# A Conformer and delta-rule trunk on one core: the second convolution's last Pool tile goes to VectorE, and the final norms' 1/rms is made with tokens on partitions

## The chip, the cores and the metric

The kernel runs on one core of a Trainium2 chip. The metric is the device time of one execution in microseconds (us), of the only core. Before the change it is 2406.96 us, the median of three runs (2406.86 to 2407.51).

## What is computed

A two-layer trunk over 1024 tokens of width 1024, all in float32. Layer 0 mixes tokens with a Conformer convolution module, layer 1 with a gated delta rule; each layer ends in a squared-ReLU MLP of width 4096, and a last RMS norm gives the output. Cut to the parts that the change touches:

```python
def conformer_conv(h, w_pw1, b_pw1, w_dw, b_dw, ln_g, ln_b, w_pw2, b_pw2):
    u = h @ w_pw1 + b_pw1
    u = jax.nn.glu(u, axis=-1)
    u = causal_depthwise_conv(u, w_dw) + b_dw
    u = jax.nn.silu(layer_norm(u, ln_g, ln_b))
    return u @ w_pw2 + b_pw2
def sqrelu_mlp(h, w1, w2):
    return jnp.square(jax.nn.relu(h @ w1)) @ w2
...
    return rms_norm(h, final_norm_g)
```

The depthwise convolution has 31 taps per channel; `rms_norm` multiplies by `rsqrt(mean(x*x) + eps)`, taken over the 1024 channels of a token.

## The kernel before

Activations lie with channels on partitions: a tensor of 512 tokens (one half `hf` of the sequence) is eight tiles of 128 channels by 512 tokens, counted by `ct`, `o` or `k`. Every matrix product is made in three passes for accuracy: weights and activations are each split into a high part and a low rest. `weights` (L161, L162) loads a raw 128x1024 block of weights, ScalarE copies it to `wh` (L161) and VectorE makes the rest `wl` (L162). `product` then issues, for each of eight k, a matmul of `wh` with the high activations (L201), of `wh` with the low ones (L202) and of `wl` with the high ones (L203): 24 matmuls. `wh` and `wl` have two buffers each (`WB = 2`), and blocks are prepared two products ahead (`AHEAD = 2`), so the block for product n+2 can be made only when product n has been issued through to its end.

Work that is not a product runs as Python generators behind the products; `tick()` advances them. The Tile scheduler turns this into one fixed order of instructions per engine, and each engine keeps to its order: an instruction that waits holds all behind it.

The second half's convolution (`hf = 1`) runs behind the MLP of layer 0, first half. That MLP is four quarters q of eight products into the hidden layer (`m1_00_q0` to `m1_00_q7`, in `mlp_hid`) and eight out of it (`m2_00_q0` to `m2_00_q7`, in `mlp_out`). After an `m1` product ScalarE takes ReLU, square and the high part (L591, L592, L102) and VectorE the low rest (L103); after an `m2` product VectorE scales (L622) and adds (L365).

The table `CONV` says which engine makes each of the eight convolution tiles. `"v"` is `conv_vec`: one multiply on VectorE (L510), then 30 fused multiply-adds (L517), as tiles `ca` and `c`. `"p"` is `conv_pool`: one ScalarE step, then 30 pairs on Pool of a multiply (L441) and an add (L446), as tiles `cv` and `cp`. The second number is the pace: how many taps between two yields. In half 1, tiles 0, 1 and 7 are Pool's. A finished tile is added to a running sum `ln1` (`conv_done`, L424).

`layer_norm(1, ...)` (from L531) starts when all eight tiles are done: mean by a matmul over the channels (`mean_lnm1`), eight subtractions on VectorE (L540), squares on ScalarE (L272) added up on Pool (L543), the variance by a matmul (`lnv1`, L548), square root on ScalarE (L247), a 128x512 reciprocal on VectorE (L248), eight products with it, four on VectorE (L560) and four on Pool (L558), fifteen or sixteen silu steps on ScalarE (L568, L569), and the split (L570). The first half's layer norm does the reciprocal in another form: `add_stats` (L254) puts tokens on partitions, so that square root and reciprocal work on 128x4 elements, and `rstd_of_tokens` brings the result back with a broadcast copy (L264) and four transposes (L267).

`final` makes the last norm: for the first half of the tokens over 512 columns, for the second half over two pieces of 256. Squares (L1006, L1010), mean by two matmuls (L1012, L1013), square root (L1016), reciprocal (L1017), then eight products and eight output DMAs. In the last piece, tiles 1, 4 and 7 go through ScalarE (L1022) and Pool (L1024), the others through VectorE (L1026).

Of the kernel before, what the change touches and what calls it, by code (L numbers as in the profile page):

```python
# [7 lines left out]
F32 = mybir.dt.float32  # L8
# [6 lines left out]
P = 128  # L15
# [15 lines left out]
        (("p", 1), ("p", 1), ("v", 3), ("v", 1), ("v", 1), ("v", 3), ("v", 1), ("p", 3)))  # L31
# [22 lines left out]
def _body(ctx, tc, a, out):  # L54
# [196 lines left out]
    def add_stats(ps, x, first=True, last=True):  # L251

        for t in range(NCH):
            nc.tensor.matmul(ps[:, t:t + 1], x[:, t * P:(t + 1) * P], mean_w[:, 0:1],  # L254
                             start=first and t == 0, stop=last and t == NCH - 1)

    def rstd_of_tokens(ps, name):

        rs = sp.tile([P, NCH], F32, tag="rs", name=f"rs_{name}", bufs=2)
        nc.scalar.activation(out=rs, in_=ps[:, :NCH], func=AF.Sqrt, bias=eps[:, 0:1], scale=1.0)  # L260
        nc.vector.reciprocal(rs, rs)
        r = g_tile(f"rstd_{name}")[:, :HT]
        r3 = r.rearrange("p (c t) -> p c t", c=NCH)
        nc.vector.tensor_copy(r3, rs.unsqueeze(2).to_broadcast([P, NCH, P]))  # L264
        pt = pg.tile([P, NCH, P], F32, tag="pg", name=f"rt_{name}")
        for t in range(NCH):
            nc.tensor.transpose(pt[:, t, :], r3[:, t, :], ident)  # L267
# [731 lines left out]
    def final(hf, cols=slice(0, HT)):  # L999
# [3 lines left out]
        ms = pg.tile([P, HT], F32, tag="pg", name=f"mean_{nm}")[:, :n]  # L1003
# [8 lines left out]
        nc.tensor.matmul(ms, mean_w, acc, start=True, stop=False)  # L1012
        nc.tensor.matmul(ms, mean_w, sq, start=False, stop=True)  # L1013
        yield
        r = g_tile(f"rstd_{nm}")[:, :n]
        nc.scalar.activation(out=r, in_=ms, func=AF.Sqrt, bias=eps[:, 0:1], scale=1.0)  # L1016
        nc.vector.reciprocal(r, r)  # L1017
        for k in range(KC):
            y = g_tile(f"fo{nm}{k}")[:, :n]
            if cols.start and k % 3 == 1:  # L1020

                nc.scalar.activation(out=y, in_=hs[hf][k][:, cols], func=AF.Copy,  # L1022
                                     scale=col["g_fin"][:, k:k + 1])
                nc.gpsimd.tensor_tensor(out=y, in0=y, in1=r, op=ALU.mult)  # L1024
            else:
                nc.vector.scalar_tensor_tensor(out=y, in0=hs[hf][k][:, cols],  # L1026
                                               scalar=col["g_fin"][:, k:k + 1], in1=r,
                                               op0=ALU.mult, op1=ALU.mult)
# [215 lines left out]
```

## Time and profile before

| what | value |
|---|---|
| median of 3 runs | 2406.96 us (2406.86 to 2407.51) |
| the profiled execution's own time | 2405.7 us |
| its span in the trace | 2403.9 us, so 1.8 us lie around it |
| mean granted TensorE clock | 0.987 of full |
| busy: TensorE, VectorE, ScalarE, Pool | 2325.9, 1607.0, 1085.4, 568.1 us |
| Pool in the second convolution | busy without a break from 283 to 598 us |

All times in the text are from the start of the span. A busy time is the sum over an engine's instructions; a TensorE row's "idle before" is what its program lost there, and the engine named behind the arrow is the one whose signal came last.

### The profile page before, as it was taken

How to read it: one execution, taken by the hardware profiler on the slowest of the kernel's cores; microseconds unless marked ns; L12 is line 12 of the kernel's file. 1: busy time of each engine (PE TensorE's matmuls, PEld its weight loads, DVE VectorE, ACT ScalarE, POOL GpSimd, SP SyncE). 2: the span in 40 equal slices, each digit the busy share in tenths (PEclk: the TensorE clock that was granted, in tenths of full speed). 3: DMA queues.
4: the chain of work that ended last, by engine and by line, in shares of the span. 5: the costliest groups of instructions: out<-in, count | busy, mean ns of one | idle time of the engine just before them, and what ended most of it. 6: DMA issues, size and time to landing. Idle time of an engine off the chain costs nothing. (4 is left out here: it accounts for less than half of the span.)

```text
span 2403.9 us, 30301 instructions
## 1 busy us (share of the span) xinstructions
PE 2325.9 (97%) x11428; PEld 1920.3 (80%) x11428; DVE 1607.0 (67%) x2648; ACT 1085.4 (45%) x1579; POOL 568.1 (24%) x411
## 2 busy tenths in 40 slices
PE   7898999999999989999999999899999999999998
PEld 5776778888778878888888888788888887888888
DVE  7897999546768978776444689786774446533334
ACT  7765433234546545352434465543524244432342
POOL 5955499999200010000000000101000000000000
PEclk9998999999999999999999999999999999999999
DMA  6545223332434534333344345443323343333332
GB/s 214 169 153 169 80 78 105 97 97 88 145 106 158 166 119 141 97 121 104 97 140 144 115 146 175 125 132 103 123 91 100 130 127 102 130 98 97 97 104 79
DMA packets 117714, 292.16 MB, mean 122 GB/s; under 512 B 29312, under 2 KB 31552, under 8 KB 117568
## 3 DMA queue, kind: packets, MB, share of 16 engines
q1 hardware_dynamic: 117568, 290.24, 38.3%
q8 instruction: 89, 1.46, 0.2%
q14 instruction: 57, 0.47, 0.1%
HBM read 250.31 MB, written 39.88 MB: 121 GB/s over the span
## 5 line engine op out<-in xcount | busy, mean ns | idle before, releaser
L161 ACT ACTIVATE wh_m<-raw_m 128x1024 fp32r<-128x1024 f32 x256 | 271.2, 1061 | 767.7 <-PE ps_m L202 690.9
L162 DVE TENSOR_TENSOR wl_m<-raw_m,wh_m 128x1024 fp32r<-128x1024 f32 x256 | 325.6, 1272 | 225.4 <-ACT wh_m L161 217.3
L203 PE MATMUL ps_m<-hid,wl_m 128*128 128x512 f32 (+1 forms) x1088 | 415.0, 383 | 9.6 <-DVE wl_m L162 9.4
L201 PE MATMUL ps_m<-hid,wh_m 128*128 128x512 f32 (+1 forms) x1088 | 414.5, 382 | 1.9 <-ACT wh_m L161 0.9
L202 PE MATMUL ps_m<-hid,wh_m 128*128 128x512 f32 (+1 forms) x1088 | 413.2, 381 | 0.0
L446 POOL TENSOR_TENSOR cp<-cp,cv 128x512 f32<-128x512 f32 x184 | 270.5, 1481 | 47.1 <-ACT cv L444 42.1
L203 PEld LDWEIGHTS ps_m<-hid,wl_m 128*128 128x128 f32 x1088 | 206.1, 189 | 50.7 <-DVE wl_m L162 14.3
L201 PEld LDWEIGHTS ps_m<-hid,wh_m 128*128 128x128 f32 x1088 | 205.9, 189 | 40.1 <-ACT wh_m L161 2.7
L202 PEld LDWEIGHTS ps_m<-hid,wh_m 128*128 128x128 f32 x1088 | 206.0, 189 | 36.9 <-issue 0.2
L201 PE MATMUL ps_m<-xn_b,wh_m 128*128 128x512 f32 x512 | 201.3, 393 | 1.0 <-ACT wh_m L161 1.0
L201 PE MATMUL ps_m<-xn_a,wh_m 128*128 128x512 f32 x512 | 200.9, 392 | 1.2 <-ACT wh_m L161 1.2
L202 PE MATMUL ps_m<-xn_a,wh_m 128*128 128x512 f32 x512 | 200.8, 392 | 0.0
L203 PE MATMUL ps_m<-xn_a,wl_m 128*128 128x512 f32 x512 | 200.8, 392 | 0.0
L202 PE MATMUL ps_m<-xn_b,wh_m 128*128 128x512 f32 x512 | 200.6, 392 | 0.0
L203 PE MATMUL ps_m<-xn_b,wl_m 128*128 128x512 f32 x512 | 200.4, 392 | 0.0
L517 DVE SCALAR_TENSOR_TENSOR ca<-u,vec,ca 128x512 f32<-128x512 f32 x267 | 185.8, 743 | 0.5
L441 POOL TENSOR_SCALAR cv<-u,vec 128x512 f32<-128x512 f32 x90 | 175.3, 1954 | 0.0
L1024 POOL TENSOR_TENSOR fof<-fof,rstd_f 128x256 f32<-128x256 f32 x3 | 2.6, 892 | 580.9 <-DVE rstd_f L1017 580.9
L818 POOL TENSOR_TENSOR ld<-qe,ld 128x512 f32<-128x512 f32 x16 | 21.6, 1351 | 455.7 <-ACT qe L788 268.2
L103 DVE TENSOR_TENSOR hid<-mt,hid 128x512 fp32r<-128x512 f32 x128 | 98.1, 767 | 43.1 <-ACT hid L102 42.9
L201 PEld LDWEIGHTS ps_m<-xn_b,wh_m 128*128 128x128 f32 x512 | 96.2, 188 | 21.8 <-ACT wh_m L161 1.8
L201 PEld LDWEIGHTS ps_m<-xn_a,wh_m 128*128 128x128 f32 x512 | 96.2, 188 | 21.5 <-ACT wh_m L161 2.1
(366 smaller groups left out, 4723.7 us busy)
## 6 DMA issues: line engine op xcount, KB each, us to landing
raw_m<-w SPq DMA_DIRECT2D x256, 512.0 KB, 3.6
raw_in<-w_in SPq DMA_DIRECT2D x64, 512.0 KB, 3.6
sc<-iy SPq DMA_DIRECT2D x64, 256.0 KB, 2.1
ld<-sc SPq DMA_DIRECT2D x64, 256.0 KB, 4.0
raw_p<-w_pw SPq DMA_DIRECT2D x16, 512.0 KB, 3.6
raw_go<-w_out SPq DMA_DIRECT2D x16, 512.0 KB, 3.6
raw_pa<-w_pw SPq DMA_DIRECT2D x15, 512.0 KB, 4.3
raw_pb<-w_pw SPq DMA_DIRECT2D x15, 512.0 KB, 4.3
```

What stands on the lines that cost most here:

```text
L103: nc.vector.tensor_tensor(out=dst[:, 1, :], in0=src, in1=dst[:, 0, :].bitcast(F32), op=ALU.subtract)
L161: nc.scalar.activation(out=wh[:, s], in_=raw[:, s], func=AF.Copy)
L162: nc.vector.tensor_tensor(out=wl[:, s], in0=raw[:, s], in1=wh[:, s].bitcast(F32), op=ALU.subtract)
L201: nc.tensor.matmul(o, wh[:, s], hi, start=(k == 0), stop=False)
L202: nc.tensor.matmul(o, wh[:, s], lo, start=False, stop=False)
L203: nc.tensor.matmul(o, wl[:, s], hi, start=False, stop=last)
L441: nc.gpsimd.tensor_scalar(out=t, in0=u[:, j:j + HT], scalar1=tap(ct, j), scalar2=None, op0=ALU.mult)
L446: nc.gpsimd.tensor_tensor(out=c, in0=c, in1=t, op=ALU.add)
L517: nc.vector.scalar_tensor_tensor(out=c if j == n - 1 else acc, in0=u[:, j:j + HT], scalar=tap(ct, j), in1=acc, op0=ALU.mult, op1=ALU.add)
L818: nc.gpsimd.tensor_tensor(out=qT[h], in0=qe, in1=qT[h], op=ALU.mult)
L1024: nc.gpsimd.tensor_tensor(out=y, in0=y, in1=r, op=ALU.mult)
```

## The change

Tile 7 of the second convolution goes from Pool (`"p"`) to VectorE (`"v"`), with a pace of two taps. `final` makes its mean with `add_stats` and its 1/rms with `rstd_of_tokens`, both now with a number of columns `n`; the 1/rms is then read from PSUM. All eight products of the last piece are VectorE's.

```diff
--- before.py
+++ after.py
@@ -28,7 +28,7 @@
 
 
 CONV = ((("s", 1), ("v", 1), ("a", 2), ("v", 1), ("a", 2), ("v", 1), ("s", 1), ("t", 1)),
-        (("p", 1), ("p", 1), ("v", 3), ("v", 1), ("v", 1), ("v", 3), ("v", 1), ("p", 3)))
+        (("p", 1), ("p", 1), ("v", 3), ("v", 1), ("v", 1), ("v", 3), ("v", 1), ("v", 2)))
 SHARED = {0: 19, 6: 17}
 DIAG = 16
 WB = 2
@@ -248,22 +248,22 @@
         nc.vector.reciprocal(r, r)
         return r
 
-    def add_stats(ps, x, first=True, last=True):
-
-        for t in range(NCH):
+    def add_stats(ps, x, first=True, last=True, n=NCH):
+
+        for t in range(n):
             nc.tensor.matmul(ps[:, t:t + 1], x[:, t * P:(t + 1) * P], mean_w[:, 0:1],
-                             start=first and t == 0, stop=last and t == NCH - 1)
-
-    def rstd_of_tokens(ps, name):
-
-        rs = sp.tile([P, NCH], F32, tag="rs", name=f"rs_{name}", bufs=2)
-        nc.scalar.activation(out=rs, in_=ps[:, :NCH], func=AF.Sqrt, bias=eps[:, 0:1], scale=1.0)
+                             start=first and t == 0, stop=last and t == n - 1)
+
+    def rstd_of_tokens(ps, name, n=NCH):
+
+        rs = sp.tile([P, NCH], F32, tag="rs", name=f"rs_{name}", bufs=2)[:, :n]
+        nc.scalar.activation(out=rs, in_=ps[:, :n], func=AF.Sqrt, bias=eps[:, 0:1], scale=1.0)
         nc.vector.reciprocal(rs, rs)
-        r = g_tile(f"rstd_{name}")[:, :HT]
-        r3 = r.rearrange("p (c t) -> p c t", c=NCH)
-        nc.vector.tensor_copy(r3, rs.unsqueeze(2).to_broadcast([P, NCH, P]))
-        pt = pg.tile([P, NCH, P], F32, tag="pg", name=f"rt_{name}")
-        for t in range(NCH):
+        r = g_tile(f"rstd_{name}")[:, :n * P]
+        r3 = r.rearrange("p (c t) -> p c t", c=n)
+        nc.vector.tensor_copy(r3, rs.unsqueeze(2).to_broadcast([P, n, P]))
+        pt = pg.tile([P, NCH, P], F32, tag="pg", name=f"rt_{name}")[:, :n]
+        for t in range(n):
             nc.tensor.transpose(pt[:, t, :], r3[:, t, :], ident)
         return pt.rearrange("p c t -> p (c t)")
 
@@ -1000,7 +1000,7 @@
         nm = f"f{hf}_{cols.start}"
         n = cols.stop - cols.start
         acc = None
-        ms = pg.tile([P, HT], F32, tag="pg", name=f"mean_{nm}")[:, :n]
+        ms = pg.tile([P, HT], F32, tag="pg", name=f"mean_{nm}")
         for k in range(KC):
             sq = g_tile(f"sq_{nm}{k}")[:, :n]
             nc.scalar.activation(out=sq, in_=hs[hf][k][:, cols], func=AF.Square)
@@ -1009,23 +1009,15 @@
             elif k < KC - 1:
                 nc.vector.tensor_tensor(out=acc, in0=acc, in1=sq, op=ALU.add)
             yield
-        nc.tensor.matmul(ms, mean_w, acc, start=True, stop=False)
-        nc.tensor.matmul(ms, mean_w, sq, start=False, stop=True)
+        add_stats(ms, acc, True, False, n // P)
+        add_stats(ms, sq, False, True, n // P)
         yield
-        r = g_tile(f"rstd_{nm}")[:, :n]
-        nc.scalar.activation(out=r, in_=ms, func=AF.Sqrt, bias=eps[:, 0:1], scale=1.0)
-        nc.vector.reciprocal(r, r)
+        r = rstd_of_tokens(ms, nm, n // P)
         for k in range(KC):
             y = g_tile(f"fo{nm}{k}")[:, :n]
-            if cols.start and k % 3 == 1:
-
-                nc.scalar.activation(out=y, in_=hs[hf][k][:, cols], func=AF.Copy,
-                                     scale=col["g_fin"][:, k:k + 1])
-                nc.gpsimd.tensor_tensor(out=y, in0=y, in1=r, op=ALU.mult)
-            else:
-                nc.vector.scalar_tensor_tensor(out=y, in0=hs[hf][k][:, cols],
-                                               scalar=col["g_fin"][:, k:k + 1], in1=r,
-                                               op0=ALU.mult, op1=ALU.mult)
+            nc.vector.scalar_tensor_tensor(out=y, in0=hs[hf][k][:, cols],
+                                           scalar=col["g_fin"][:, k:k + 1], in1=r,
+                                           op0=ALU.mult, op1=ALU.mult)
             c0 = hf * HT + cols.start
             nc.sync.dma_start(out[k * P:(k + 1) * P, c0:c0 + n], y)
             yield
```

The scheduler makes a new order from this. Before the first step of the new tile, at 318 us, it is the old one. From there to the end of the layer-0 MLP, tiles and norm steps stand elsewhere on VectorE, ScalarE and Pool; from the second `pw2` on only a few neighbours are swapped, until `final`.

First place: VectorE in the third quarter of the MLP, when the third and fourth `m1` weights are made (names are tile_layer-half_quarter-product, the last number is a counter). Before:

```order
L162 TENSOR_TENSOR wl_m1_00_22_3891<-raw_m1_00_22_3888,wh_m1_00_22_3890 128x1024
L103 TENSOR_TENSOR hid_00_20_3875<-mt_00_20_3872,hid_00_20_3875 128x512
L162 TENSOR_TENSOR wl_m1_00_23_3948<-raw_m1_00_23_3945,wh_m1_00_23_3947 128x1024
L103 TENSOR_TENSOR hid_00_21_3932<-mt_00_21_3929,hid_00_21_3932 128x512
L162 TENSOR_TENSOR wl_m1_00_24_4005<-raw_m1_00_24_4002,wh_m1_00_24_4004 128x1024
L103 TENSOR_TENSOR hid_00_22_3989<-mt_00_22_3986,hid_00_22_3989 128x512
L162 TENSOR_TENSOR wl_m1_00_25_4053<-raw_m1_00_25_4050,wh_m1_00_25_4052 128x1024
```

Now:

```order
L162 TENSOR_TENSOR wl_m1_00_22_3835<-raw_m1_00_22_3832,wh_m1_00_22_3834 128x1024
L103 TENSOR_TENSOR hid_00_20_3828<-mt_00_20_3825,hid_00_20_3828 128x512
L162 TENSOR_TENSOR wl_m1_00_23_3874<-raw_m1_00_23_3871,wh_m1_00_23_3873 128x1024
L424 TENSOR_TENSOR ln1_3081<-ln1_3081,cp1_1_3083 128x512
L103 TENSOR_TENSOR hid_00_21_3867<-mt_00_21_3864,hid_00_21_3867 128x512
L424 TENSOR_TENSOR ln1_3081<-ln1_3081,c1_4_3308 128x512
L424 TENSOR_TENSOR ln1_3081<-ln1_3081,c1_5_3934 128x512
L424 TENSOR_TENSOR ln1_3081<-ln1_3081,c1_6_4153 128x512
L162 TENSOR_TENSOR wl_m1_00_24_3913<-raw_m1_00_24_3910,wh_m1_00_24_3912 128x1024
```

The last four additions to `ln1` now stand here, ahead of `wl_m1_00_24`, and the first of them reads tile 1, which is Pool's. Before, they stood some 110 us later.

Second place: VectorE at the end of the same quarter's `m1` products, around the layer norm's reciprocal. Before, these steps stood in the fourth quarter's `m2` products:

```order
L162 TENSOR_TENSOR wl_m2_00_33_4918<-raw_m2_00_33_4915,wh_m2_00_33_4917 128x1024
L248 RECIPROCAL rstd_ln1_5018<-rstd_ln1_5018 128x512
L281 TENSOR_TENSOR sq_a20_5197<-sq_a20_5197,sq_a21_5212 128x512
L560 SCALAR_TENSOR_TENSOR cp1_0_2398<-cp1_0_2398,vec_97,rstd_ln1_5018 128x512
L622 TENSOR_TENSOR xo_00_32_4950<-ps_m2_00_32_4921,rstd_r2_2760 128x512
L560 SCALAR_TENSOR_TENSOR c1_2_2393<-c1_2_2393,vec_97,rstd_ln1_5018 128x512
L560 SCALAR_TENSOR_TENSOR c1_4_3308<-c1_4_3308,vec_97,rstd_ln1_5018 128x512
L560 SCALAR_TENSOR_TENSOR c1_6_4246<-c1_6_4246,vec_97,rstd_ln1_5018 128x512
L162 TENSOR_TENSOR wl_m2_00_34_4960<-raw_m2_00_34_4957,wh_m2_00_34_4959 128x1024
```

Now:

```order
L162 TENSOR_TENSOR wl_m2_00_20_4089<-raw_m2_00_20_4086,wh_m2_00_20_4088 128x1024
L248 RECIPROCAL rstd_ln1_5073<-rstd_ln1_5073 128x512
L103 TENSOR_TENSOR hid_00_26_4080<-mt_00_26_4077,hid_00_26_4080 128x512
L560 SCALAR_TENSOR_TENSOR cp1_0_2398<-cp1_0_2398,vec_97,rstd_ln1_5073 128x512
L560 SCALAR_TENSOR_TENSOR c1_2_2393<-c1_2_2393,vec_97,rstd_ln1_5073 128x512
L560 SCALAR_TENSOR_TENSOR c1_4_3308<-c1_4_3308,vec_97,rstd_ln1_5073 128x512
L560 SCALAR_TENSOR_TENSOR c1_6_4153<-c1_6_4153,vec_97,rstd_ln1_5073 128x512
L162 TENSOR_TENSOR wl_m2_00_21_4132<-raw_m2_00_21_4129,wh_m2_00_21_4131 128x1024
```

Reciprocal and four products stand ahead of `wl_m2_00_21`, where they stood ahead of `wl_m2_00_34`.

Third place: ScalarE at the start of the fourth quarter's `m2` products. Before:

```order
L102 ACTIVATE hid_00_37_4824<-mt_00_37_4821 128x512
L272 ACTIVATE sq_ln10_4829<-cp1_0_2398 128x512
L272 ACTIVATE sq_ln11_4854<-cp1_1_3083 128x512
L272 ACTIVATE sq_ln12_4870<-c1_2_2393 128x512
L272 ACTIVATE sq_ln13_4896<-c1_3_2643 128x512
L272 ACTIVATE sq_ln14_4912<-c1_4_3308 128x512
L272 ACTIVATE sq_ln15_4938<-c1_5_4026 128x512
L272 ACTIVATE sq_ln16_4954<-c1_6_4246 128x512
L272 ACTIVATE sq_ln17_4980<-cp1_7_3744 128x512
L161 ACTIVATE wh_m2_00_32_4875<-raw_m2_00_32_4873 128x1024
L161 ACTIVATE wh_m2_00_33_4917<-raw_m2_00_33_4915 128x1024
```

Now, from the last silu steps of a row of fifteen (the rows above them are the table load after `hid_00_37` and eight steps of L568):

```order
L568 ACTIVATE la17_5112<-c1_7_4718,vec_97 128x512
L569 ACTIVATE cp1_0_2398<-cp1_0_2398,vec_97 128x512
L569 ACTIVATE cp1_1_3083<-cp1_1_3083,vec_97 128x512
L569 ACTIVATE c1_2_2393<-c1_2_2393,vec_97 128x512
L569 ACTIVATE c1_3_2643<-c1_3_2643,vec_97 128x512
L569 ACTIVATE c1_4_3308<-c1_4_3308,vec_97 128x512
L569 ACTIVATE c1_5_3934<-c1_5_3934,vec_97 128x512
L569 ACTIVATE c1_6_4153<-c1_6_4153,vec_97 128x512
L161 ACTIVATE wh_m2_00_32_4779<-raw_m2_00_32_4777 128x1024
L569 ACTIVATE c1_7_4718<-c1_7_4718,vec_97 128x512
L161 ACTIVATE wh_m2_00_33_4817<-raw_m2_00_33_4815 128x1024
```

Between `hid_00_37` and `wh_m2_00_32` eight squares stood before; a table load and fifteen silu steps stand there now. The squares stand in the third quarter's `m1` products now, between `hid_00_23` and `wh_m1_00_26`.

## Rows read from the trace of the kernel before

**Rows 1.** Waits of TensorE from 240 to 720 us: total, times, longest.
```profile
PE ps_m L203 <- DVE wl_m L162: 6.8, 4, 2.8
```
**Rows 2.** Timeline of TensorE, 340 to 362 us: start, us, engine, line, [idle before].
```profile
345.56 0.50 PE L203 MATMUL ps_m<-hid,wl_m 128*128 128x512 f32 x1 [2.06 <-DVE wl_m L162]
...
359.53 0.50 PE L203 MATMUL ps_m<-hid,wl_m 128*128 128x512 f32 x1 [1.61 <-DVE wl_m L162]
```
**Rows 3.** Timeline of VectorE, 336 to 362 us.
```profile
336.72 5.35 DVE L517 SCALAR_TENSOR_TENSOR ca<-u,vec,ca 128x512 f32<-128x512 f32 x8
...
343.84 1.67 DVE L162 TENSOR_TENSOR wl_m<-raw_m,wh_m 128x1024 fp32r<-128x1024 f32 x1
```
**Rows 4.** Timeline of Pool, 460 to 470 and 557 to 598 us.
```profile
462.42 1.29 POOL L446 TENSOR_TENSOR cp<-cp,cv 128x512 f32<-128x512 f32 x1
...
465.24 2.09 POOL L446 TENSOR_TENSOR cp<-cp,cv 128x512 f32<-128x512 f32 x1
...
572.62 25.26 POOL L446 TENSOR_TENSOR cp<-cp,cv 128x512 f32<-128x512 f32 x15
```
**Rows 5.** Timeline of TensorE: two matmuls around the start of `m1_00_24`.
```profile
490.62 0.39 PE L201 MATMUL ps_m<-xn_a,wh_m 128*128 128x512 f32 x1
...
491.07 0.39 PE L203 MATMUL ps_m<-xn_a,wl_m 128*128 128x512 f32 x1
```
**Rows 6.** Timeline of TensorE, 612 to 631 us, in the fourth quarter's `m2` products.
```profile
613.43 0.50 PE L201 MATMUL ps_m<-hid,wh_m 128*128 128x512 f32 x1 [0.47 <-ACT wh_m L161]
...
614.68 1.13 PE L548 MATMUL lnv<-sq_ln,mean_w 128*128 128x512 f32 x2 [0.52 <-POOL sq_ln L543]
...
629.84 0.65 PE L203 MATMUL ps_m<-hid,wl_m 128*128 128x512 f32 x1 [2.76 <-DVE wl_m L162]
630.29 0.63 PE L201 MATMUL ps_m<-hid,wh_m 128*128 128x512 f32 x1
```
**Rows 7.** Busy times by stretch: PE, PEld, DVE, ACT, POOL, then granted TensorE clock, DMA.
```profile
360.00:364.00 4.00, 4.00 (x20) 3.28 (x19) 4.00 (x8) 0.00 (x0) 3.76 (x4) 1.00 0.42 131
628.00:632.00 4.00, 2.16 (x6) 1.68 (x7) 4.00 (x6) 4.00 (x6) 0.10 (x1) 0.75 0.31 52
632.00:636.00 4.00, 4.00 (x16) 3.27 (x15) 3.13 (x5) 3.82 (x7) 0.00 (x0) 0.82 0.79 284
```
**Rows 8.** Timeline of VectorE, 617 to 630 us: the layer norm's reciprocal and products.
```profile
617.97 3.34 DVE L248 RECIPROCAL rstd_ln<-rstd_ln 128x512 f32<-128x512 f32 x1
...
624.08 4.57 DVE L560 SCALAR_TENSOR_TENSOR c<-c,vec,rstd_ln 128x512 f32<-128x512 f32 x3
628.57 1.21 DVE L162 TENSOR_TENSOR wl_m<-raw_m,wh_m 128x1024 fp32r<-128x1024 f32 x1
```
**Rows 9.** Timeline of ScalarE, 600 to 632 us: a product's eviction, then silu steps.
```profile
600.12 1.06 ACT L161 ACTIVATE wh_m<-raw_m 128x1024 fp32r<-128x1024 f32 x1 [2.57 <-PE ps_m L202]
...
602.35 0.63 ACT L102 ACTIVATE hid<-mt 128x512 fp32r<-128x512 f32 x1
...
622.58 1.28 ACT L568 ACT_TABLE_LOAD   x1
623.87 1.43 ACT L568 ACTIVATE la<-cp,vec 128x512 fp32r<-128x512 f32 x2
...
630.39 1.04 ACT L161 ACTIVATE wh_m<-raw_m 128x1024 fp32r<-128x1024 f32 x1
```
**Rows 10.** Timeline of all engines, 225 to 229 us: the first half's 1/rms.
```profile
225.42 1.05 PE L254 MATMUL lnv<-mean_w,sq_ln 128*128 128x1 f32 x8 [2.83 <-DVE sq_ln L543]
...
227.59 1.09 PE L267 MATMUL rt_ln<-ident,rstd_ln 128*128 128x128 f32 x4 [1.12 <-DVE rstd_ln L264]
```
**Rows 11.** Timeline of all engines from 2393 us: the last `final`.
```profile
2393.81 0.70 PE L1013 MATMUL mean_f<-sq_f,mean_w 128*128 128x256 f32 x2 [0.23 <-ACT sq_f L1006]
...
2396.84 3.47 DVE L1026 SCALAR_TENSOR_TENSOR fof<-hn,vec,rstd_f 128x256 f32<-128x256 f32 x5
...
2397.35 4.16 SPq L1030 DMA_DIRECT2D out<-fof  x8
```

## The prediction

> **What bounds the kernel now.** I first read the page's busy times: TensorE works nearly the whole span, so the time is its work plus its gaps. The waits of TensorE from 240 to 720 us, around the stretch that the change reorders, show which gaps: the largest sum is that of L203 on VectorE's `wl`, 6.8 us in 4 waits [rows 1]. TensorE's timeline gives three of these: 2.06 and 1.61 us while the convolution's taps fill VectorE [rows 2], 2.76 us in the second layer norm [rows 6]. Last come the timelines of VectorE, ScalarE and Pool there, for what stood ahead of the late weights, and the end of the kernel. The rows show a rhythm: two matmuls start 0.45 us apart [rows 5], so a product of 24 lasts 5.44. The next weights but one may be made only when a product ends, by ScalarE in 1.06 [rows 9] and VectorE in 1.21 [rows 8], and the low part is wanted 5.44 + 0.45 = 5.89 us after that. So **a burst of more than 5.89 - 2.27 = 3.6 us on either engine, ahead of a weight, stops TensorE**. This is the yardstick for every moved step.
>
> About 0.2% (4.8 us) is what a measurement here can tell from no change.
>
> **The change, part by part.**
>
> *Taps.* Pool loses 60 operations of tile 7. It works beside TensorE, so this alone gives nothing. VectorE gains one multiply and 30 taps. A tap takes 0.66 us (eight in 5.35 [rows 3]), so about 20.5 us in all. From 309 to 419 us VectorE is busy throughout; behind this it is about half idle, and most of the taps go there. What costs is the order in front of the two weights for which TensorE waits today. Counted in the new order, the first of them (start 343.84 [rows 3]) has two more operations ahead, 1.4 us, and the second one more after that, 0.65. Both already come last at their matmul [rows 2], so both delays are TensorE's: **+2.0**. It can't be below 1.4, and is 4.0 if three more weights slip by a tap each, since VectorE has no idle time there.
>
> *The wait for Pool.* VectorE now takes Pool's tile 1 into the sum ahead of `wl_m1_00_24`. Pool's sixteenth add of that tile ends at 467.3 [rows 4]. Fourteen remain, without the multiplies of tile 7 between them. Undisturbed one is 1.29 us, in the run of fifteen it was 25.26/15 = 1.68 [rows 4], so Pool ends between 485.4 and 490.9. I take 490: VectorE still works beside it until it stops to wait. Behind the waiting add stand a hidden tile, three more adds and `wl_m1_00_24`; five adds of 0.6 make 493.0. TensorE wants the mean at 491.07 [rows 5], after two matmuls, plus the 2.0 us by which it is now late: 493.1. The two meet, so **+0.4**, between 0 and 1.5. Mean, subtractions, squares and Pool's sums then lie beside three products; I cost them at nothing, as the variance is asked for two products later.
>
> *Reciprocal and products ahead of `wl_m2_00_21`.* Let S be the start of product `m1_00_27`. The variance matmuls are done at S + 1.6 (two matmuls and 1.13 [rows 6]), ScalarE's root at S + 2.4, the reciprocal of 3.34 [rows 8] at S + 5.8. A hidden tile and four products follow. Before, four such products and one 0.6 us step filled the time from the reciprocal's end to 628.57, with another 0.6 [rows 8]: 7.3 us, or 6.8 with one 0.6 step. So `wl_m2_00_21` is ready at S + 5.8 + 6.8 + 1.2 = S + 13.8. TensorE wants it after `m1_00_27` with the variance (6.3), one product and two matmuls: S + 12.2. Gap 1.6. The granted clock after a gap of 1.61 stayed 1.00, full speed, of 2.4 GHz [rows 2, 7]; after one of 2.76 us it was 0.75 and 0.82 in the next two stretches, so part of them ran at 1.2 GHz, with matmuls 0.45 instead of 0.23 apart [rows 6, 7]: 4 x (0.25 + 0.18) = 1.7 us. I add 0.4 for the chance of that here: **+2.0**, between 0 and 3.4.
>
> *Fifteen silus ahead of `wh_m2_00_32`.* Let T be the start of `m2_00_30`. ScalarE makes a weight and three steps of an eviction: from 600.12 to 602.98 [rows 9], T + 2.9. The table load takes 1.28. Between its end and the next weight, ten silus took 630.39 - 623.87 = 6.52 [rows 9], 0.65 each, so fifteen take 9.8. The weight's high part is ready at T + 15.0, its low part at T + 16.2. TensorE wants them at T + 10.9 and T + 11.3: gap **4.9**. It is 3.7 if a silu costs as little as a square there, 0.6. After 4.9 us of idle the clock falls as it did after 2.76, **+1.7**, or 0 if it doesn't.
>
> A rule speaks against this step. The trace shows the first silu at 623.87 behind a load that began at 622.58 and lasted 1.28 [rows 9]: nothing between. The Trainium skill (ScalarE: Activation LUTs, What ACT_TABLE_LOAD costs) puts about 1.38 us of drain behind each load, an estimate of 1.4 us more for this gap, 2414.4 in all. The trace does not agree, and the sum goes by the trace.
>
> The clock's price has its page too. The Trainium skill (TensorE: Matmul & The Clock Gate, Part 1) says that idling halves the clock and that sustained work restores it. By that rule, the trace agrees after 2.76 us; after 1.61 us the row shows no fall.
>
> *What goes.* The old episode in the fourth quarter: 0.47, 0.52 and 2.76 us of gaps [rows 6] and the 1.7 of clock, with less than 0.1 between: **-5.5**. It can be no more, and is 3.8 if the clock falls nearby anyway.
>
> *The norms.* The mean costs TensorE about the same in both forms. The transposes are new: four in 1.09 [rows 10], and two in half of that, inserted among products: **+1.5** for the first two `final`s, between 1.0 and 2.0. In the last one, from the mean of the last square to the first product 2393.81 to 2396.84 = 3.0 us passed [rows 11]. The first half's layer norm went the new way in 225.42 to 228.68 = 3.3 us [rows 10], for eight statistics matmuls and four transposes; here half of each is needed, some 0.9 less: 2.4. The eight outputs were issued in 4.16 us [rows 11], by SP's queue, not by Pool's products; without Pool, 0.3 to 0.4 less. **-1.0**, between -0.5 and -1.3. The DMA count doesn't change.
>
> Sum: 2.0 + 0.4 + 2.0 + 6.6 - 5.5 + 1.5 - 1.0 = **+6.0**. The profiled execution is 2405.7 (span 2403.9 and 1.8 around it), 1.3 below the median of 2406.96; on the median the sum makes **2413.0 us**.
>
> **The rivals.**
>
> *The idle time takes it up.* VectorE and ScalarE are half idle from 420 to 600 us, and the layer norm comes there from a crowded place. If TensorE's gaps around Pool's end, the reciprocal and the silus all close, only -5.5 - 1.0 + 1.5 = -5.0 is left: 2402.0, faster. It decides at the 3.6 us yardstick: bursts must be shorter than that. The first place passes it; for the two others I count 10 and 11 us in one piece [rows 8, 9]. Against it.
>
> *A smaller stall.* Silus at 0.6, no fall of the clock, the reciprocal's burst hidden by a TensorE that is late: 2.0 + 0.4 + 3.7 - 5.5 + 1.5 - 1.0 = +1.1, 2408.1, no change that can be told. For it: the clock stayed full after 1.61. Against: 3.7 is above 2.76.
>
> *VectorE falls behind.* If the four-tap rhythm delays every weight to 440 us, the taps cost 4.0, Pool 1.5, and each stall the clock: 4.0 + 1.5 + 3.4 + 6.6 - 5.5 + 1.5 - 1.0 = +10.5, 2417.5. For it: VectorE has no idle time from 320 to 420. Against: the counts ahead of the later weights hardly grow.
>
> That the change doesn't move what it says can be left out, as the orders show the moves.
>
> **How the numbers follow.** Forecast 0.42, the large stall 0.08, the small one 0.33, taken up 0.17. The first two are slower by over 0.2%: 0.50; the third is the same; the fourth is faster. The range goes from 2401, where all is taken up and the norms and the last stretch take their better ends (0.5 and 0.3 less), to 2419, 1.5 above the largest case. The likeliest case's own range is 2410 to 2416.
>
> **What would show it.** In the new trace: a TensorE gap of 4 to 5 us about 10.9 us after the fourth quarter's `m2` products start, at the third weight, with a row of fifteen silus on ScalarE, and a lower clock behind it; a gap near 1.6 at the second `m2` weight of the third quarter, behind four products on VectorE; 3.4 and 2.3 us where 2.06 and 1.61 stood. No gap at the old place. The last DMA about 1 us nearer to the last matmul. It is wrong if the silus lie between weights, if VectorE waits for Pool well after 491, or if the gaps add up to less than 3 us.

## The result and the profile after

| | before | after |
|---|---|---|
| median of 5 runs each, measured together | 2406.86 us (2401.91 to 2407.51) | 2416.94 us (2414.21 to 2418.92) |
| the profiled execution's own time, its span | 2405.7, 2403.9 | 2418.92, 2417.1 |
| mean granted clock | 0.987 | 0.984 |

The changed kernel is slower: the ratio is 1.005, with a 95% interval from 1.0039 to 1.006, so 9 to 14 us. Forecast were 2413.0 us, slower, in a range from 2401 to 2419. The profiled execution is the slowest of the five; its span is 13.2 us above the one of before.

First the page's part 1 of the changed kernel: busy time, share and instructions of each engine.

```profile
PE 2332.0 (96%) x11456; PEld 1926.8 (80%) x11456; DVE 1615.8 (67%) x2685; ACT 1081.7 (45%) x1575; POOL 464.1 (19%) x348
```

Pool has lost 104 us of work, VectorE has gained 9, and TensorE, which bounds the kernel, has 6 us more "busy". Its 28 more matmuls don't make these: the final norms alone, run further down, have them too, at 2325.5 us. They are put down to matmuls at the lower clock, which last longer. The waits of TensorE say more. This is the changed kernel from 240 to 735 us (waiting engine and line, releaser, total us, times, longest):

```profile
PE ps_m L203 <- DVE wl_m L162: 9.6, 6, 2.7
PE ps_m L201 <- ACT wh_m L161: 8.2, 9, 4.1
...
PE ps_m L201 <- DVE xo L622: 1.7, 1, 1.7
```

The first line was 6.8 us in 4 waits [rows 1]. The second, for ScalarE's high parts, was 2.2 us in 4 waits. One wait for `xo` was 0.5 us. The timeline of TensorE in the same kernel shows the places (start, us, idle before):

```profile
334.04 0.50 PE L203 MATMUL ps_m<-hid,wl_m 128*128 128x512 f32 x1 [0.78 <-DVE wl_m L162]
...
347.63 0.47 PE L201 MATMUL ps_m<-hid,wh_m 128*128 128x512 f32 x1 [1.66 <-DVE xo L622]
350.99 0.80 PE L203 MATMUL ps_m<-hid,wl_m 128*128 128x512 f32 x1 [2.66 <-DVE wl_m L162]
364.96 0.50 PE L203 MATMUL ps_m<-hid,wl_m 128*128 128x512 f32 x1 [1.27 <-DVE wl_m L162]
...
446.08 0.50 PE L203 MATMUL ps_m<-hid,wl_m 128*128 128x512 f32 x1 [2.45 <-DVE wl_m L162]
...
533.55 0.50 PE L203 MATMUL ps_m<-hid,wl_m 128*128 128x512 f32 x1 [2.21 <-DVE wl_m L162]
540.21 0.50 PE L201 MATMUL ps_m<-hid,wh_m 128*128 128x512 f32 x1 [0.47 <-ACT wh_m L161]
...
631.15 0.50 PE L201 MATMUL ps_m<-hid,wh_m 128*128 128x512 f32 x1 [4.07 <-ACT wh_m L161]
632.80 0.80 PE L201 MATMUL ps_m<-hid,wh_m 128*128 128x512 f32 x1 [0.86 <-ACT wh_m L161]
```

Where 2.06 and 1.61 stood [rows 2] there are now four gaps. The one before 446.08 has no counterpart at all: before, TensorE was busy all the time from 420 to 480 us, and VectorE only half of it (PE, PEld, DVE, ACT, POOL busy, then clock and DMA):

```profile
420.00:480.00 60.00, 60.00 (x265) 49.36 (x265) 30.48 (x30) 17.53 (x22) 60.00 (x36) 1.00 0.31 97
```

The gaps before 533.55 and 631.15 are the two that were forecast, of the reciprocal and of the silus; the old episode [rows 6] is gone.

Gaps alone don't give the time, since the clock falls behind some of them. So the same matmul is set beside itself in both traces: the n-th L201 matmul, counted from 0, of which every kernel here has 3136. The table gives how much later it starts than in the trace of before, less the difference at the 300th (270 us), where no kernel differs in order yet; in the changed kernel that difference is 1.3 us of the 13.2 between the spans. Under each place stands its time in the trace of before.

```
n of L201      408    500    560    632    700    760    780    820    900   3100
before, us   351.6  416.9  458.0  506.9  553.9  594.7  609.6  644.7  705.6 2378.8
after        +4.44  +4.06  +9.38 +11.15 +14.57 +14.57 +12.79 +13.56 +13.56 +12.65
no taps      +3.52  +2.15  +2.55  +4.32  +9.35  +9.35  +7.58  +7.26  +7.19  +4.72
taps extra   +3.76  +3.49  +8.77  +8.77  +8.68 +13.21 +12.89 +10.23 +10.30 +10.56
late tile 7  -0.02  -0.06  -0.00  +1.54  +5.77  +5.77  +3.99  +3.81  +3.89  +2.23
silus early  +4.33  +4.07  +9.44 +11.21 +16.14 +16.14 +14.37  +7.17  +7.11  +5.17
tokens       +4.29  +4.12  +9.44 +11.21 +12.35 +12.35 +10.58 +10.73 +10.73  +8.52
all three    -0.01  -0.05  -0.05  +1.49  +4.09  +4.09  +2.31  -4.89  -4.87  -8.60
norms alone  -0.04  -0.07  -0.03  -0.03  -0.03  -0.03  -0.03  +0.05  +0.05  -3.13
no Pool      +2.67  +4.01  +5.78  +8.83  +8.32  +8.32  +6.55  +6.81  +6.89  +3.99
```

The row of the change reads: 4.1 us in the convolution's first stretch, 5.3 at 443 us, 1.8 for the mean's matmuls, which come back as -1.8 before 780, 3.4 around the reciprocal, of which 0.9 are the variance's matmuls, and at last the silus against the old episode, +0.8, with those 0.9 given back in it. From 705 us on the row of the change falls by 0.9 us and other rows by up to 3.7, a large part of it at one place near 1748 us: VectorE's late weight stops TensorE there for 1.80 us in the trace of before, with a fall of the clock behind it (0.70 from 1748 to 1752), for 1.07 us without one in the changed kernel, and for 2.49 us without one in the norms alone. With a single trace of most kernels nothing is read from that part.

### The profile page after: what moved, and what is told of

Read it like the earlier page. It is cut to its first block, busy times and chain, and to the rows that moved or that the text cites. A ratio compares the mean times of both kernels' runs of the same rounds, so it can differ in the third digit from the quotient of the medians.

```text
span 2417.1 us, 30315 instructions
## 1 busy us (share of the span) xinstructions
PE 2332.0 (96%) x11456; PEld 1926.8 (80%) x11456; DVE 1615.8 (67%) x2685; ACT 1081.7 (45%) x1575; POOL 464.1 (19%) x348
## 4 chain that ended last, share of the span: by engine, by line
PE 80%; DVE 9%; ACT 3%; DMA 3%; issue 3%; POOL 1%; SPq 1%; DVEq 0%; POOLq 0%; ACTq 0%
PE ps_m L203 18%; PE ps_m L201 18%; PE ps_m L202 17%; PE ps_in L201 3%; PE ps_in L203 3%; PE ps_in L202 3%; DVE ca L517 2%; POOL cp L446 1%; PE ps_go L201 1%; PE ps_go L203 1%; PE ps_go L202 1%; PE ps_p L203 1%; PE ps_p L201 1%; PE ps_p L202 1%; DVE wl_m L162 1%
## 5 line engine op out<-in xcount | busy, mean ns | idle before, releaser
L162 DVE TENSOR_TENSOR wl_m<-raw_m,wh_m 128x1024 fp32r<-128x1024 f32 x256 | 323.2, 1263 | 226.0 <-ACT wh_m L161 218.7
L201 PE MATMUL ps_m<-hid,wh_m 128*128 128x512 f32 (+1 forms) x1088 | 415.2, 382 | 9.3 <-ACT wh_m L161 7.0
L201 PEld LDWEIGHTS ps_m<-hid,wh_m 128*128 128x128 f32 x1088 | 206.4, 190 | 49.3 <-ACT wh_m L161 10.1
L446 POOL TENSOR_TENSOR cp<-cp,cv 128x512 f32<-128x512 f32 x154 | 227.9, 1493 | 47.6 <-ACT cv L444 42.5
L517 DVE SCALAR_TENSOR_TENSOR ca<-u,vec,ca 128x512 f32<-128x512 f32 x296 | 205.5, 746 | 2.0 <-issue 1.5
L201 PE MATMUL ps_m<-xn_a,wh_m 128*128 128x512 f32 x512 | 201.0, 392 | 1.2 <-ACT wh_m L161 1.2
L201 PE MATMUL ps_m<-xn_b,wh_m 128*128 128x512 f32 x512 | 201.1, 393 | 0.5 <-ACT wh_m L161 0.5
L103 DVE TENSOR_TENSOR hid<-mt,hid 128x512 fp32r<-128x512 f32 x128 | 93.0, 727 | 45.0 <-ACT hid L102 44.6
L201 PEld LDWEIGHTS ps_m<-xn_a,wh_m 128*128 128x128 f32 x512 | 96.2, 188 | 21.9 <-ACT wh_m L161 2.1
L203 PEld LDWEIGHTS ps_m<-xn_a,wl_m 128*128 128x128 f32 x512 | 96.2, 188 | 21.1 <-DVE wl_m L162 1.1
L365 DVE TENSOR_TENSOR hn<-hn,ps_m 128x512 f32<-128x512 f32 x56 | 38.4, 686 | 111.0 <-PE ps_m L203 110.9
L201 PEld LDWEIGHTS ps_m<-xn_b,wh_m 128*128 128x128 f32 x512 | 96.2, 188 | 20.3 <-ACT wh_m L161 0.9
```

What stands on the lines that cost most here:

```text
L103: nc.vector.tensor_tensor(out=dst[:, 1, :], in0=src, in1=dst[:, 0, :].bitcast(F32), op=ALU.subtract)
L162: nc.vector.tensor_tensor(out=wl[:, s], in0=raw[:, s], in1=wh[:, s].bitcast(F32), op=ALU.subtract)
L201: nc.tensor.matmul(o, wh[:, s], hi, start=(k == 0), stop=False)
L203: nc.tensor.matmul(o, wl[:, s], hi, start=False, stop=last)
L365: nc.vector.tensor_tensor(out=hs[hf][o], in0=hs[hf][o], in1=ps, op=ALU.add)
L446: nc.gpsimd.tensor_tensor(out=c, in0=c, in1=t, op=ALU.add)
```

## Experiments

The theory after these traces: the loss lies wholly between 320 and 650 us, most of it where VectorE is filled with taps (T). Against it stood that the layer norm's early place carries it (L), and that the new final norms have a good part (B).

**The change in two halves.** First tile 7 alone:

```diff
-        (("p", 1), ("p", 1), ("v", 3), ("v", 1), ("v", 1), ("v", 3), ("v", 1), ("p", 3)))
+        (("p", 1), ("p", 1), ("v", 3), ("v", 1), ("v", 1), ("v", 3), ("v", 1), ("v", 2)))
```

> 

> Only tile 7's move from Pool to VectorE; the final norms as before. Theory A (the loss is all in the MLP of layer 0, by VectorE's filled stretch and the early layer norm): +12 to +14 us against before. Theory B (the new final norms cost a good part): +6 to +8 us.

Measured: 2418.3 us beside 2403.53 of before, ratio 1.0061 (1.0049 to 1.0074), 12 to 18 us. Then the final norms alone, which is the change with the line above undone:

> 

> Only the final norms in the token form, with VectorE making all last products; tile 7 stays on Pool. Theory A: between -1.5 and 0 us. Theory B, and my own sum on record for this part (+1.5 for the transposes, -1.0 at the end): +0.5 us or more.

Measured: 2402.89 beside 2403.53, ratio 0.9997 (0.9988 to 1.0006): no difference that can be told. As far as these runs tell, all of the loss is tile 7's.

**Taps or layer norm.** One kernel takes the taps away and leaves the early end of Pool, the other adds the taps and leaves Pool as it was.

```diff
-            for j in range(1, n):
+            for j in range(n - 1 if (hf, ct) == (1, 7) else 1, n):
```

> 

> The change, but of tile 7's 30 taps on VectorE 29 are left out (the tile holds the first and the last tap alone), so Pool ends as early as in the change and the layer norm comes early, with no more VectorE work than before. Theory T (VectorE's filled stretch carries most of the loss): the gaps near 333, 349 and 443 us fall back to the 2.06 and 1.61 of before, the row of fifteen silus still costs 4.9 us and a fall of the clock against the old episode's 5.5, so +1 to +3 us. Theory L (the layer norm's early place carries it): +7 to +9 us.

Measured: 2410.86, ratio 1.0029 (1.0018 to 1.0041), 4 to 10 us.

```diff
-        for ct in conv_of(hf, "vst"):
+        for ct in conv_of(hf, "vst") + ([7] if hf else []):
...
-            n = own_taps(hf, ct)
+            n = CW if hf else own_taps(hf, ct)
...
+            if hf and ct == 7:
+                continue
             if lack:
```

(with tile 7 `"p"` again, and its input kept for both)

> 

> The change, but Pool still makes tile 7 and its result is the one used; VectorE makes the 31 taps of tile 7 as well, for nothing. So VectorE's stretch is as full as in the change and the layer norm stays at its old place. Theory T: the gaps near 333, 349 and 443 us are those of the change, +8 to +10 us, with the old episode at 612 to 634 us back. Theory L: 0 to +2 us.

Measured: 2414.55, ratio 1.0048 (1.0035 to 1.006), 8 to 14 us. Taken by itself the first run speaks for L, since it lies above T's 1 to 3 us, and the second for T: both theories have a share, and the shares overlap. In the table, taps without the early layer norm cost 8.8 us by 458 us; the early layer norm without taps costs 4.6 us from 458 to 705.6, and without the taps some 2.5 us are left in the first stretch, where the order is still another one than before. Theory T's gap near 443 us is gone without the taps, and with them it is there in its old size, 2.42 for 2.45 us:

```profile
444.12 0.50 PE L203 MATMUL ps_m<-hid,wl_m 128*128 128x512 f32 x1 [2.42 <-DVE wl_m L162]
```

That is TensorE's timeline with the taps extra. Without the taps the forecast of 1 to 3 us was still too low: the gap at the reciprocal was 2.33 us there, and this time the clock fell behind it (4.1 us between the 632nd and the 700th matmul beyond the 0.9 of the variance).

**Amount or order of the taps.** In the changed kernel VectorE is busy without a break from 310 to 451 us, before from 309 to 419. This is its timeline ahead of the gap at 443:

```profile
433.63 1.21 DVE L162 TENSOR_TENSOR wl_m<-raw_m,wh_m 128x1024 fp32r<-128x1024 f32 x1
434.76 1.40 DVE L517 SCALAR_TENSOR_TENSOR ca<-u,vec,ca 128x512 f32<-128x512 f32 x2
436.08 0.68 DVE L103 TENSOR_TENSOR hid<-mt,hid 128x512 fp32r<-128x512 f32 x1
436.68 5.35 DVE L517 SCALAR_TENSOR_TENSOR ca<-u,vec,ca 128x512 f32<-128x512 f32 x8
441.95 0.68 DVE L622 TENSOR_TENSOR xo<-ps_m,rstd_r 128x512 f32<-128x512 f32 x1
...
443.81 3.35 DVE L162 TENSOR_TENSOR wl_m<-raw_m,wh_m 128x1024 fp32r<-128x1024 f32 x2
```

Between the two weights stand eleven taps, 7.3 us, where a product lasts 5.44. Ten of them stand ahead of the first of two `xo`, which need the products just made, and one between the two. VectorE reached the `xo` late, without a wait before them, and the weight behind came too late for TensorE. The next kernel gives tile 7 a false need of tile 4's result:

```diff
-            if n == CW:
+            if (hf, ct) == (1, 7):
+                nc.vector.scalar_tensor_tensor(out=acc, in0=cs[1][4], scalar=0.0,
+                                               in1=col["b_dw"][:, ct:ct + 1].to_broadcast([P, HT]),
+                                               op0=ALU.mult, op1=ALU.add)
+            elif n == CW:
...
-            for j in range(1, n):
+            for j in range(0 if (hf, ct) == (1, 7) else 1, n):
```

> 

> The change, but the first step of tile 7 on VectorE reads tile 4's result (times zero) and so waits for it; the same number of taps then runs three at a time, and tile 7's behind 419 us, where VectorE has idle time. One more operation of 0.66 us. If it is the order of the taps in the filled stretch that costs: the gap of 2.45 us near 443 us and its fall of the clock go (5.3 us), and the stretch from 320 to 365 us goes back by 2 to 4, so +4 to +7 us against before, what is left being the layer norm's early place. If the 20 us of added VectorE work cost wherever they stand: +10 us or more.

Measured: 2406.15 beside 2403.81, ratio 1.0009 (1.0 to 1.0018), so at most 4 us: better than expected. The table shows the first two losses gone whole (-0.06 at the 500th matmul, -0.00 at the 560th), with one operation more on VectorE. The later ones stay: 5.8 us from the 560th to the 700th matmul, where the changed kernel loses 5.2, the layer norm's own matmuls in both. At the place of the gap near 443 us VectorE now waits for TensorE, not TensorE for it; its timeline in this kernel:

```profile
433.18 0.69 DVE L626 TENSOR_TENSOR xo<-ps_m,rstd_r 128x512 f32<-128x512 f32 x1 [4.51 <-PE ps_m L203]
433.90 0.82 DVE L365 TENSOR_TENSOR h<-h,xo 128x512 f32<-128x512 f32 x1
434.65 1.21 DVE L162 TENSOR_TENSOR wl_m<-raw_m,wh_m 128x1024 fp32r<-128x1024 f32 x1
```

So up to 458 us the amount of added work costs nothing; when it is done costs 9.4 us. No run tried another pace for tile 7. Why was VectorE late? From 321 to 449, with Pool busy beside it, some of its operations are drawn out, by 9.7 us against the shortest of their kind in that stretch, or by 12.6 if the shortest of the whole trace is taken for all but the taps. The test takes Pool away:

```diff
-            for j in range(j0 + 1, CW):
+            for j in range(CW if hf else j0 + 1, CW):
```

> 

> The change, but Pool's 30 pairs for each of tiles 0 and 1 of half 1 are left out (those tiles hold one tap), so VectorE makes its tiles alone. Only the stretch up to 450 us is to be read; the layer norm comes earlier than in any other kernel. In the change VectorE's operations between 321 and 449 us are together 12.6 us longer than their shortest forms. If this slowing beside Pool is what makes VectorE late: the gap of 0.78 near 333 and the 2.45 near 443 us go or fall below 1. If the order of the taps alone does it: they stay within 0.5 of 0.78 and 2.45.

A single execution took 2406.81 us, which isn't used. TensorE has no gap near 443 us: it is busy 59.99 of 60 us from 400 to 460, where the changed kernel has 56.86. Both rows of the view by stretch (PE, PEld, DVE, ACT, POOL busy, then clock), first without Pool, then the changed kernel:

```profile
400.00:460.00 60.00, 59.99 (x261) 48.70 (x260) 53.63 (x71) 26.47 (x37) 11.45 (x7) 1.00 0.28 90
```

```profile
400.00:460.00 60.00, 56.86 (x242) 45.94 (x241) 55.44 (x73) 21.63 (x29) 60.00 (x36) 0.97 0.29 92
```

VectorE has idle time there, ahead of weights too. The loss of the first stretch isn't gone: the row without Pool stands at +4.0 at the 500th matmul, as the changed kernel's does, and the next 1.8 are the mean's matmuls. The gap near 333 is gone there, but one of 1.92 us before 360.6 stays, ones of 1.24 before 308.2 and 1.87 before 317 are new, and the clock fell behind the two longer ones (0.70 from 360 to 364, 0.66 from 316 to 320). So without Pool the gap near 443 us is gone, and what is lost before it is as much as ever. The order isn't quite the same: eight taps and a sum stand between the two weights here. VectorE then waits 1.87 us for TensorE, which the three taps more (2.0 us) would just have filled:

```profile
435.24 0.68 DVE L424 TENSOR_TENSOR ln<-ln,c 128x512 f32<-128x512 f32 x1
437.79 1.29 DVE L622 TENSOR_TENSOR xo<-ps_m,rstd_r 128x512 f32<-128x512 f32 x2 [1.87 <-PE ps_m L203]
```

So the order of the change has nothing to spare there. That the slowing beside Pool is what it lacked fits this run but isn't shown apart from the three taps. With three tiles at a time VectorE has the slack, with four beside Pool it hasn't.

**The two stalls of the layer norm.** ScalarE's timeline in the changed kernel at the fourth quarter's `m2` products:

```profile
618.25 0.63 ACT L102 ACTIVATE hid<-mt 128x512 fp32r<-128x512 f32 x1
618.90 1.28 ACT L568 ACT_TABLE_LOAD   x1
620.20 1.43 ACT L568 ACTIVATE la<-cp,vec 128x512 fp32r<-128x512 f32 x2
621.53 4.05 ACT L568 ACTIVATE la<-c,vec 128x512 fp32r<-128x512 f32 x6
625.49 1.42 ACT L569 ACTIVATE cp<-cp,vec 128x512 f32<-128x512 f32 x2
626.81 3.34 ACT L569 ACTIVATE c<-c,vec 128x512 f32<-128x512 f32 x5
630.06 1.04 ACT L161 ACTIVATE wh_m<-raw_m 128x1024 fp32r<-128x1024 f32 x1
```

Their inputs were ready from 533 us on. The edit does each silu once, in place, and lets Pool copy it:

```diff
-            if k % 2 and small:
+            if hf or k % 2:
                 nc.scalar.activation(out=c[k], in_=c[k], func=AF.Silu, bias=b, scale=g)
                 nc.gpsimd.tensor_copy(act[k][:, 0, :], c[k])
```

> 

> The change, but in half 1 each silu is done once, in place, and Pool copies it into the product's operand. Theory: the fifteen silus stood in one row because half of them write operand tiles that come free only when the last m1 product of the quarter has ended; in place they need none and go up to where ScalarE is idle. Then the gap of 4.07 + 0.86 us and its fall of the clock go: 6 to 7 us less than the change, +6 to +8 against before. If the row was only ScalarE's amount of work: 1 to 3 us less than the change.

Measured: 2410.99, ratio 1.0032 (1.0021 to 1.0044), +5 to +11, which holds the +6 to +8 of the first theory. The other figure, 6 to 7 us less than the change, the medians don't show: 7.2 beside 10.1 over before is 3 us less, which the second theory gave too. The traces decide. The gaps of 4.07 and 0.86 us are gone, and in the table the step from the 780th to the 820th matmul goes from +0.8 to -7.2; 1.6 us more than in the changed kernel are lost ahead of it, around the reciprocal, so by the 820th matmul it is 6.4 us less. The silus have moved up some 90 us, right behind the products with 1/rms, among the evictions:

```profile
526.81 1.28 ACT L565 ACT_TABLE_LOAD   x1
528.10 1.43 ACT L565 ACTIVATE cp<-cp,vec 128x512 f32<-128x512 f32 x2
529.44 0.71 ACT L565 ACTIVATE c<-c,vec 128x512 f32<-128x512 f32 x1
530.05 0.61 ACT L592 ACTIVATE mt<-mt 128x512 f32<-128x512 f32 x1
530.57 2.77 ACT L565 ACTIVATE c<-c,vec 128x512 f32<-128x512 f32 x4
```

The copies into the operand tiles, now Pool's, take the place of what was held up: they start at 617.38, when the quarter's last `m1` product has ended. That the operand tiles came free only then fits this; no run gave the kernel more of these tiles.

The other stall, with the second half's layer norm in the first half's form:

```diff
-            if k == KC - 1 and small:
+            if k == KC - 1:
                 add_stats(v, sq)
...
-        if small:
-            r = rstd_of_tokens(v, f"ln{hf}")
-        else:
-            r = rstd(v, f"ln{hf}")
+        r = rstd_of_tokens(v, f"ln{hf}")
```

(and all eight products on VectorE)

> 

> The change, but the second half's layer norm makes its 1/rms with tokens on partitions as the first half's does, all eight products on VectorE, none on Pool. If the 3.34 us reciprocal makes the 2.21 us gap near 531 us: that gap and the 0.47 behind it go, 2 to 3 us less than the change (+9 to +12 against before). If the products behind it make the gap: 0 to 1 us less.

Measured: 2412.85, ratio 1.0036 (1.0023 to 1.0048), 5 to 12 us above before. In the table the step from the 632nd to the 700th matmul falls from 3.4 to 1.1: 2.3 less, as expected. The edit takes away both the long reciprocal and Pool's share of the products, so it doesn't tell their shares apart.

**All three edits.**

> 

> The change with the three edits together: tile 7 behind tile 4, silus in place, layer norm in token form. If the three stalls are all there is to the loss, the old episode's 5.5 us and the 0.7 of the final norms are left as a gain, less 1 to 2 us in the first stretch: -3 to -6 us against before. If the stalls only move on: +2 us or more.

Measured: 2396.56 beside 2403.81, ratio 0.9972 (0.9961 to 0.9982), 4 to 9 us faster than before; the median, 7.3, lies above the 3 to 6 that were expected. In the table 4.9 are gained by 705 us, and the rest lies in the part from which nothing is read. TensorE's waits from 300 to 720 us are down to this:

```profile
PE ps_m L203 <- DVE wl_m L162: 4.7, 4, 2.0
PE ps_p L201 <- ACT wh_p L161: 1.5, 2, 1.0
PE ps_m L201 <- DVE xo L618: 0.5, 1, 0.5
PE ps_m L201 <- ACT wh_m L161: 0.5, 1, 0.5
```

Is tile 7's move then worth anything? The same kernel with tile 7 on Pool (`("p", 3)`):

> 

> As the kernel with the three edits, but tile 7 stays on Pool with its pace of three: final norms and second layer norm in token form, silus in place. It tells whether moving tile 7 is worth anything once the rest is mended. If the old episode is only the reciprocal and the silus: -4 to -6 us against before, as good as the three edits. If the layer norm still crowds the fourth quarter's m2 products: -1 to -3 us.

Measured: 2398.29, ratio 0.9981 (0.9972 to 0.999), 2 to 7 us faster: the median, 5.4, lies in the first of the two cases, the interval reaches into the second. Both once more, on one chip:

> 

> The kernel with the three edits once more, on one chip with the next, to set the two side by side: 6 to 7 us faster than before.

> 

> Tile 7 on Pool and all else mended, beside the run above. By the traces so far TensorE's gaps from 300 to 720 us sum to 7.2 us with tile 7 behind tile 4 on VectorE and to 8.4 here, and the old place of the layer norm costs no fall of the clock: 1 to 2 us slower than the run above. If the move is worth nothing: within 0.5 us.

Measured: 2396.06, ratio 0.9967 (0.9955 to 0.998), and 2398.07, ratio 0.9972 (0.9961 to 0.9983). The move gains some 2 us in both pairs of medians and in both pairs of spans (2393.7 and 2393.7 beside 2395.7 and 2395.9), but the intervals overlap. Most of the gain comes with the layer norm's new form and its early silus, which need no move.

## Why the prediction was right in its direction and short in its size

The terms are read here from one pair of traces; they sum to 12.9 us, where the medians are 10.1 apart.

*Taps, +2.0: measured 9.4.* This is the term that was mis-sized, and by far the most. It is the price of the order that the moved tile brings: without its taps 2.5 of it stay, with the tile held back none. The first stretch cost 4.1, just past the upper bound of 4.0, and not as the forecast's 3.4 and 2.3 us of gaps: four gaps of 6.4 us in all stood for 3.7. The prediction gave this term no clock, and of this place it had read only the row behind the 1.61 us. Behind the 2.06 us the clock had fallen in the trace of before too, and in the changed kernel it fell for longer. Before, then the changed kernel:

```profile
348.00:352.00 4.00, 4.00 (x14) 3.18 (x14) 4.00 (x6) 0.00 (x0) 4.00 (x4) 0.73 0.50 162
```

```profile
350.00:354.00 4.00, 3.01 (x7) 2.43 (x8) 4.00 (x6) 0.00 (x0) 4.00 (x3) 0.50 0.47 136
```

The 5.3 at 443 us (2.45 + 0.47 + 0.21 of gaps and the lower clock behind) was costed at nothing. The sentences that failed are "behind this it is about half idle, and most of the taps go there" and, against the third rival, "the counts ahead of the later weights hardly grow". The taps did go there, but a half idle engine hides work only if that work stands behind the weight that TensorE asks for next; eleven taps stood ahead of it. The prediction had read two places of the new order on VectorE and not the switch from `m1` to `m2` products in the second quarter, which has the shape of the first place that it did read. The rival that VectorE falls behind, with a chance of 0.08, was the nearest to what happened: its 10.5 us were made of 4.0 for the taps and more elsewhere, its mechanism was the right one, at one more place.

*Pool, +0.4: measured 0.* Pool's run of adds in the changed kernel, and VectorE's wait for it:

```profile
468.83 26.43 POOL L446 TENSOR_TENSOR cp<-cp,cv 128x512 f32<-128x512 f32 x15
```

```profile
495.30 0.69 DVE L424 TENSOR_TENSOR ln<-ln,cp 128x512 f32<-128x512 f32 x1 [2.56 <-POOL cp L446]
```

VectorE waited 2.56 us, to 495.30. By the prediction's own signs a wait well after 491 spoke against it; but TensorE was 10.7 us late by then, and took up the mean at 501.79 without a gap. Pool ended past the 485.4 to 490.9 of the forecast; with a TensorE late by 2.0 us, and so asking at 493.1, these rows would make a wait. That the term came to nothing is luck: the lateness from the taps hid it.

*Reciprocal, +2.0: measured 2.5.* Forecast was a gap of 1.6 with a part of a fall of the clock; it was 2.21 and 0.47 behind it, with no fall (1.00 from 532 to 540). The order and the burst were as worked out. VectorE's timeline in the changed kernel:

```profile
521.66 3.35 DVE L248 RECIPROCAL rstd_ln<-rstd_ln 128x512 f32<-128x512 f32 x1
524.93 0.63 DVE L103 TENSOR_TENSOR hid<-mt,hid 128x512 fp32r<-128x512 f32 x1
525.48 1.78 DVE L560 SCALAR_TENSOR_TENSOR cp<-cp,vec,rstd_ln 128x512 f32<-128x512 f32 x1
527.18 5.18 DVE L560 SCALAR_TENSOR_TENSOR c<-c,vec,rstd_ln 128x512 f32<-128x512 f32 x3
532.28 1.21 DVE L162 TENSOR_TENSOR wl_m<-raw_m,wh_m 128x1024 fp32r<-128x1024 f32 x1
```

*Silus, 4.9 of gap and 1.7 of clock: measured 4.93 and 3.3.* The gap is right to a few hundredths, though its second part waited for the next weight's high part and not for the low part. (The 3.7 for the small case doesn't follow from silus of 0.6 us; fifteen of these take 9.0 for 9.8, which makes 4.1.) The clock cost twice as much: the 32 L201 matmuls of four products, from 621.48 to 651.43, took 29.95 us for 21.76 of work; 8.2 are lost, 4.93 of them in gaps. The changed kernel's clock by stretch:

```profile
628.00:632.00 4.00, 0.80 (x2) 0.30 (x2) 4.00 (x8) 4.00 (x7) 0.00 (x0) 0.96 0.47 133
632.00:636.00 4.00, 3.20 (x8) 2.48 (x9) 3.81 (x5) 1.79 (x3) 0.00 (x0) 0.50 0.54 159
636.00:640.00 4.00, 4.00 (x14) 3.19 (x13) 0.00 (x0) 0.00 (x0) 0.00 (x0) 0.69 0.50 167
```

From 632 to 636 all was at 1.2 GHz, where it was 0.82 behind the old 2.76 us [rows 7].

On the table load, the Trainium skill (ScalarE: Activation LUTs, What ACT_TABLE_LOAD costs) puts some 1.38 us of drain behind it; here the first silu started at 620.20 behind a load from 618.90 of 1.28, and the gap came out without that drain. The measurement decides.

*The old episode, -5.5: measured about -6.4,* by the same count over three products. It did go.

*Norms, +1.5: measured about 0; the end, -1.0: measured -0.8.* Between the 2300th and the 2800th L201 matmul the changed kernel loses nothing against before, and the kernel with the final norms alone confirms it. A gap of 0.47 that stood at 2061.9 us is gone with the old form; what else paid for the transposes stays open, so this +1.5 is a term that no run here shows. The last mean and 1/rms in the changed kernel, with the first product at 2410.48 (the old way is in [rows 11]):

```profile
2407.86 1.05 PE L254 MATMUL mean_f<-mean_w,sq_f 128*128 128x1 f32 x8 [0.85 <-DVE sq_f L1010]
...
2409.88 0.56 PE L267 MATMUL rt_f<-ident,rstd_f 128*128 128x128 f32 x2 [0.97 <-DVE rstd_f L264]
2410.48 3.22 DVE L1018 SCALAR_TENSOR_TENSOR fof<-hn,vec,rt_f 128x256 f32<-128x256 f32 x8 [0.74 <-PE rt_f L267]
```

*The number.* That 2416.94 lies inside the range is in part luck. The top of the range, 2419, was built from a fall of the clock behind the reciprocal and a longer wait for Pool, and neither came. The loss on the taps, 7.4 us more than the forecast, and the 1.6 more of the silus' clock were partly paid back by the norms' +1.5 and by 0.9 more from the old episode. The direction was not luck: tile 7's move alone makes the kernel slower, and the largest single stall came where and about as large as it was forecast.

## What to carry to other kernels

An engine that is half idle on average can still stop the one that bounds the kernel: what counts is what stands, in its order, ahead of the next piece that the other asks for, at every switch from one phase to the next, and whether the engine still has slack when it gets there. So walk the whole order of the stretch that a moved piece of work enters, not the places of today's waits. A false dependence of 0.66 us that keeps the moved work behind what is urgent gave back 9.4 us by 458 us, where the move itself is worth some 2 us at most; and a step that writes tiles which come free late is better split, so that its long part needs none of them.

## What the runs showed of the hardware that was not expected

- Beside Pool it was not the taps that VectorE did more slowly. From 321 to 449 us 110 taps, which read one operand from PSUM, lost 0.8 us in all against the shortest of them there; 21 weight splits (L162) lost 4.3, 12 hidden splits (L103) 1.9 and 10 additions (L365) 2.7, all with two operands in SBUF. In the kernel without Pool the means in that stretch fell from 1.41 to 1.26, from 0.84 to 0.71 and from 0.95 to 0.70 us; the taps' rose from 0.74 to 0.77, for which no run gives the cause.
- The length of a single gap of TensorE doesn't tell whether its clock falls. It fell behind 1.80 us (near 1748, before), 2.06 us (near 345, before) and 2.33 us (at the reciprocal, without taps: 0.60 from 536 to 540). It stayed at 1.00 behind 1.61 us before [rows 2, 7], and behind three longer gaps: 2.21 us in the changed kernel, 2.42 us at the same place with the early silus, and 2.35 us near 634 with the taps extra. Behind 4.07 + 0.86 us a fall cost twice what it did behind 2.76.
